# An encoder step on one core: w_out split by ACT and DVE, a shorter weight chain, w_down's maxima tied to their units, two token sums kept in SBUF

## The chip, the core and the metric

One core of a Trainium2 chip runs the whole program. Its engines are TensorE (PE, whose weight loads are shown apart as PEld), VectorE (DVE), ScalarE (ACT), GpSimd (POOL) and SyncE (SP, which here only issues DMA transfers). The metric is the device time of one execution in microseconds (us); lower is better. PE's clock is granted at one of two levels, 1.2 or 2.4 GHz; the profile gives the granted clock of a stretch as a share of the full one.

## The reference

One step of a one-layer streaming encoder on 2048 prompt tokens and 32 sample tokens, width 1024:

```python
h = h + rmsnorm(concat(y_conv, y_attn) @ W_out)
h = h + rmsnorm(relu(rmsnorm(h) @ W_up)**2 @ W_down)      # W_up 1024x4096, W_down 4096x1024
h = h + rmsnorm((p @ W_pe) * sigmoid(h @ W_g))

# differential attention, 4 heads, two softmax maps of each
a = softmax(where(visible, q k^T * scale - slope * |t - s|, -1e30))
attn = a[map 0] - lam * a[map 1]
o = rmsnorm(attn @ v, g_subln) * (1 - lam_init)
```

The attention is causal by chunks of 64 tokens; y_conv is a gated three-tap convolution.

## The kernel before, in words

Every large product is made in 16-bit floats with both operands as a high and a low half: the high half is the value rounded to 16 bits, the low half what is left, and three matmuls (high·high, low·high, high·low) go into one PSUM bank. So every weight and activation is split into halves on ACT (high, a copy with a scale, L170) and DVE (low, a scalar_tensor_tensor, L105). The weights are scaled by powers of two that come from their largest absolute value, so a reduction to the maximum stands before each split.

The program is written for a scheduler that sets the order of instructions on every engine from the dependences and from its own simulated timeline. What is written in another order, or depends on something else, can therefore move at many places.

The stages, with their time in the trace:
- 0 to 140 us: norm of the tokens and the first projections. 140 to about 975 us: attention, 4 heads of 16 units of 128 queries, woven with the other projections. A unit makes its scores (PE, L590, L591), adds the bias and takes the row maximum (DVE, L594), has the maximum negated on POOL (`nm`), exponentials with their row sums on ACT (L601), and then combines both maps. `weights_of` (L489) makes from the two row sums z1 and z2 a column of small [128,1] operations on POOL and DVE; ACT scales the second map with `sgc` (L625), DVE combines both (L105, `s<-s,sg,s`), PE transposes (`pta`), ACT and DVE split the transposed map (`at`), PE multiplies it by v (`smb`, L619, L621), and `subnorm` (L507) makes `rso` on POOL and `yg` on DVE.
- About 880 to 1135 us: 16 tiles of the product with w_out (`mix`, L897 to L901). Its eight blocks of rows are split by `split_in_place` (L175): POOL scales the block in place, ACT copies it to the high half (L176), POOL subtracts for the low half (L177). After the norm the tokens are transposed and combined to the seven sums of a Strassen-Winograd product, for two pairs of token groups. `place2` (L1206) puts the sums of the first pair (p = 0) into SBUF for good; those of the second pair go through a ring of 10 buffers (`ob`) to DRAM (`u2_d`).
- 1135 to 1777 us: w_up. 16 units, one for each block of 256 columns; a unit has two `up_pair` calls (one for each pair of tokens) of seven products, 12 matmuls each (L1301 to L1303), into a ring of three PSUM banks. `u2b` are the sums of the second pair, loaded back from DRAM (L1295). Beside unit k the `Piece` k+1 is made ready: load (`stg`), row maximum (`am`, L140), PE transpose of it (`pmx`), maximum (`p2mx`, L149), PE broadcast (`pmb`, L1154), scale (`um` to `i_u`), and the splits of the seven sums (`w7`, shown as `w`). `down_max` (L1370) loads a block of w_down (`stgd`) and reduces it to its largest absolute value (L1374); the table MAXIMA deals the 16 calls to units 2 to 13 in the order of the program text.
- 1777 to 2400 us: w_down. `raw` (L1450) loads a block, ACT and DVE split it to `v`; `fr` are the squared activations read back from DRAM, split to `hl`; L1533 to L1535 multiply. The buffers for `raw`, `fr` and `v` come from pools opened as those of the up stage close; `pva` lies in the place of the pool `pupa` (weights being prepared), the pools of `raw` and `fr` in that of `pupb`, whose `w7` the last matmuls of the up stage read.
- 2400 to 2627 us: the gate stage.

## Time and profile before

| | us |
|---|---|
| median of 3 runs | 2629.61 (2629.27 to 2631.32) |
| the profiled execution | 2628.69, of which the span of the records is 2626.9 |
| PE busy | 2532.1 (96% of the span) |
| DVE busy | 1692.2 (64%) |
| ACT busy | 1204.6 (46%) |
| POOL busy | 731.5 (28%) |

The span runs from the first to the last instruction; some 1.8 us lie outside it. PE is busy nearly all the time, so what can be found in such a profile are the stretches where PE stands (length less busy time) or runs with a granted clock below 1. Where PE stands, the list of waits says what it waited for last.

### The profile page before, as it was taken

The numbers are of one execution on the slowest core, as the hardware profiler recorded it, in microseconds if no ns is written. First come the engines' busy times: TensorE is split into PE (matmuls) and PEld (weight loads), VectorE is DVE, ScalarE is ACT, GpSimd is POOL, SyncE is SP. The second block draws the span as 40 slices with busy tenths as digits, with TensorE's granted clock in tenths as the row PEclk, the third lists the DMA queues.
The fourth block names the chain that finished last, engine by engine and source line by source line (L and its number), as shares of the span: only waits on it lengthen the run. The fifth ranks groups of instructions, "written<-read, shape, count | busy, mean of one in ns | idle before, by whom it ended". The sixth has DMA issues, their size and how long they took to land.

```text
span 2626.9 us, 42707 instructions
## 1 busy us (share of the span) xinstructions
PE 2532.1 (96%) x16495; PEld 1346.2 (51%) x16495; DVE 1692.2 (64%) x2933; ACT 1204.6 (46%) x2126; POOL 731.5 (28%) x1383
## 2 busy tenths in 40 slices
PE   8999999999999789989999999999999999999998
PEld 8755754755665444444444444443444444444454
DVE  6568858858887567886755555554563457555764
ACT  5446735744754545543343443444332223334553
POOL 2142233233222543432222222210220101233442
PEclk8999999999999899989999999999999999999999
DMA  5121111101111124577633333336753456541221
GB/s 174 50 66 38 38 33 45 52 28 57 46 62 33 61 73 153 173 279 267 205 129 124 117 125 129 117 142 243 253 194 107 145 206 225 197 139 57 93 75 60
DMA packets 215803, 315.76 MB, mean 120 GB/s; under 512 B 19184, under 2 KB 109712, under 8 KB 215600
## 3 DMA queue, kind: packets, MB, share of 16 engines
q1 hardware_dynamic: 215600, 313.04, 35.7%
q8 instruction: 129, 2.11, 0.3%
q14 instruction: 74, 0.61, 0.1%
HBM read 208.78 MB, written 100.02 MB: 118 GB/s over the span
## 4 chain that ended last, share of the span: by engine, by line
PE 61%; DVE 5%; DMA 5%; POOL 3%; ACT 2%; issue 1%; SPq 0%; DVEq 0%; POOLq 0%; ACTq 0%
PE mm L1533 6%; PE mm L1535 6%; PE mm L1534 6%; PE mm L1301 6%; PE mm L1303 6%; PE mm L1302 6%; PE mm L897 5%; PE mm L899 4%; PE mm L901 4%; DMA stgd<-in_w_down_dram 2%; PE lin L313 1%; PE lin L314 1%; PE lin L315 1%; DVE wdm L1374 1%; DMA wtmp<-in_w_pe_gate_dram 1%
## 5 line engine op out<-in xcount | busy, mean ns | idle before, releaser
L1533 PE MATMUL mm<-v,hl 128*128 128x512 f16 x896 | 340.1, 380 | 4.4 <-ACT v L170 4.4
L1535 PE MATMUL mm<-v,hl 128*128 128x512 f16 x896 | 339.9, 379 | 1.7 <-DVE hl L1495 1.5
L1534 PE MATMUL mm<-v,hl 128*128 128x512 f16 x896 | 340.0, 379 | 0.0
L313 PE MATMUL lin<-uh,whl 128*128 128x512 f16 (+1 forms) x832 | 265.6, 333 | 3.6 <-DVE ks L105 1.8
L314 PE MATMUL lin<-ul,whl 128*128 128x512 f16 (+1 forms) x832 | 265.4, 333 | 2.6 <-DVE ul L105 2.6
L315 PE MATMUL lin<-uh,whl 128*128 128x512 f16 (+1 forms) x832 | 265.2, 333 | 0.0
L1494 ACT ACTIVATE hl<-fr 128x1024 f16<-128x1024 f32 x112 | 117.5, 1051 | 319.9 <-PE mm L1535 302.5
L1495 DVE TENSOR_TENSOR hl<-fr,hl 128x1024 f16<-128x1024 f32 x112 | 144.7, 1299 | 178.1 <-ACT hl L1494 175.5
L601 ACT ACTIVATE s<-s,nm 128x128 f32<-128x128 f32 (+15 forms) x128 | 153.6, 1200 | 156.8 <-POOL nm L100 156.3
L1301 PE MATMUL mm<-u,w 128*128 128x512 f16 x448 | 171.0, 382 | 5.8 <-ACT w L170 3.8
L1301 PE MATMUL mm<-u2b,w 128*128 128x512 f16 x448 | 170.4, 382 | 2.4 <-DMA u2b<-u_d 1.3
L1302 PE MATMUL mm<-u2b,w 128*128 128x512 f16 x448 | 171.3, 382 | 0.0
L1302 PE MATMUL mm<-u,w 128*128 128x512 f16 x448 | 171.0, 382 | 0.0
L1303 PE MATMUL mm<-u,w 128*128 128x512 f16 x448 | 169.6, 381 | 1.2 <-DVE w L105 1.2
L1303 PE MATMUL mm<-u2b,w 128*128 128x512 f16 x448 | 169.9, 382 | 0.0
L1533 PEld LDWEIGHTS <-hl 128*128 128x128 f16 x896 | 87.7, 98 | 114.6 <-issue 11.0
L594 DVE CUSTOM_DVE_ANT_0 s<-sc,bias,mx 128x512 f32<-128x512 f32 (+3 forms) x192 | 135.4, 705 | 16.0 <-PE sc L591 10.8
L1535 PEld LDWEIGHTS <-hl 128*128 128x128 f16 x896 | 87.7, 98 | 109.2 <-DVE hl L1495 3.7
L1303 PEld LDWEIGHTS <-w 128*128 128x128 f16 x896 | 88.1, 98 | 108.1 <-issue 2.4
L1301 PEld LDWEIGHTS <-w 128*128 128x128 f16 x896 | 89.2, 100 | 105.0 <-ACT w L170 4.1
L1302 PEld LDWEIGHTS <-w 128*128 128x128 f16 x896 | 88.0, 98 | 104.5 <-issue 7.9
L1534 PEld LDWEIGHTS <-hl 128*128 128x128 f16 x896 | 87.7, 98 | 104.3 <-issue 0.9
(449 smaller groups left out, 6055.7 us busy)
## 6 DMA issues: line engine op xcount, KB each, us to landing
ff_d<-e SPq DMA_DIRECT2D x224, 256.0 KB, 2.0
fr<-ff_d SPq DMA_DIRECT2D x112, 512.0 KB, 4.3
raw<-in_w_down_dram SPq DMA_DIRECT2D x80, 512.0 KB, 4.5
xt<-in_x_prompt_dram SPq DMA_DIRECT2D x32, 512.0 KB, 4.1
stg<-in_w_up_dram SPq DMA_DIRECT2D x16, 1024.0 KB, 6.3
stgd<-in_w_down_dram SPq DMA_DIRECT2D x16, 1024.0 KB, 6.0
stg<-in_w_in_dram SPq DMA_DIRECT2D x24, 512.0 KB, 4.0
h_d<-ht SPq DMA_DIRECT2D x16, 512.0 KB, 2.9
```

The lines of the kernel that those rows point to most:

```text
L313: T.matmul(o, w[:, 0, ft], rh[:, ft, c], start=(ft == 0), stop=False)
L314: T.matmul(o, w[:, 0, ft], rl[:, ft, c], start=False, stop=False)
L315: T.matmul(o, w[:, 1, ft], rh[:, ft, c], start=False, stop=(ft == FT - 1))
L594: V.tensor_tensor_reduce(out=s_[:, c0:c0 + w_], in0=ps[:, :w_], in1=bias[:, b0:b0 + w_], scale=h["idd"], scalar=-BIG if prev is None else ...
L601: A.activation(out=s_[:, :nk], in_=s_[:, :nk], func=AF.Exp, bias=nm, accum_out=zz)
L1301: T.matmul(o, w[:, c, 0, kt], x[:, :, 0, kt], start=first and kt == 0, stop=False, skip_group_check=True)
L1302: T.matmul(o, w[:, c, 0, kt], x[:, :, 1, kt], start=False, stop=False, skip_group_check=True)
L1303: T.matmul(o, w[:, c, 1, kt], x[:, :, 0, kt], start=False, stop=kt == 3, skip_group_check=True)
L1495: V.tensor_tensor(out=hl[:, 1], in0=fr, in1=hl[:, 0], op=SUB)
L1533: T.matmul(ps, hl[:, 0, u % 2, c], v[:, 0], start=(u == 0), stop=False)
L1534: T.matmul(ps, hl[:, 0, u % 2, c], v[:, 1], start=False, stop=False)
L1535: T.matmul(ps, hl[:, 1, u % 2, c], v[:, 0], start=False, stop=(u == NU - 1))
```

## The change

- `weights_of`: before, 1/z2, then c = z1·nlam/z2 and 1 + alam·z1/z2, its reciprocal, and the product of both. After, d = z1·alam + z2, r = 1/d, sgc = z1·r·nlam, sg = z2·r. One DVE reciprocal and two POOL operations fewer in each of the calls.
- w_out's blocks go through `split` (L170 on ACT with the scale, L105 on DVE) in place of `split_in_place`.
- The second pair's sums for B11 and T3 have buffers of their own in SBUF (16 KB in each partition), and their stores to and loads from DRAM are gone (8 stores of 256 KB, 2 loads of 1 MB). The ring `ob` has 4 buffers in place of 10.
- The load of a `down_max` may be issued only after the store of A11 of the `up_pair` before it, its reduction only after that pair's S2 sum on DVE.
- `raw` has a ring of 3 and 1, and the first four blocks of w_down go into one buffer in `pva`; the ring of `v` changes accordingly.

```diff
     def weights_of(z1, z2, k0, rows=P):
-        rz, c, a_, sg = t1("rz"), t1("c"), t1("ca"), t1("sg")
-        V.reciprocal(out=rz[:rows], in_=z2[:rows])
-        ts(G, c[:rows], z1[:rows], rz[:rows], MUL, nlam[:rows], MUL)
-        ts(G, a_[:rows], rz[:rows], z1[:rows], MUL, alam[:rows], MUL)
-        ts(G, a_[:rows], a_[:rows], 1.0, ADD)
-        V.reciprocal(out=sg[:rows], in_=a_[:rows])
-        sgc = t1("sgc")
-        G.tensor_tensor(out=sgc[:rows], in0=sg[:rows], in1=c[:rows], op=MUL)
+        r, d, sg, sgc = t1("rz"), t1("ca"), t1("sg"), t1("sgc")
+        ts(G, d[:rows], z1[:rows], alam[:rows], MUL, z2[:rows], ADD)
+        V.reciprocal(out=r[:rows], in_=d[:rows])
+        ts(G, sgc[:rows], z1[:rows], r[:rows], MUL, nlam[:rows], MUL)
+        G.tensor_tensor(out=sg[:rows], in0=z2[:rows], in1=r[:rows], op=MUL)
         kk = t1("kk")
         if k0 is not None:
             ts(G, kk[:rows], sg[:rows], z1[:rows], MUL, k0[:rows], MUL)
...
         here["ppost"] = s_wo.enter_context(tc.tile_pool(name="ppost", bufs=1, reuse_waits="tile"))
         for r in ROWS:
             w = wo[r] = pwo.tile([P, 2, D], F16, tag="w", bufs=8, name="w")
-            split_in_place(w[:, 0], w[:, 1], out_scale["sgs"][r], out_scale["aswo" if r < 4 else "swo"])
+            split(w[:, 0], w[:, 1], out_scale["sgs"][r], out_scale["aswo" if r < 4 else "swo"])
             yield
...
     idn = cst.tile([P, 1], F32, name="idn")
     here["pupa"] = s_up.enter_context(tc.tile_pool(name="pupa", bufs=1, side="right", reuse_waits="tile"))
+    pu2r = s_up.enter_context(tc.tile_pool(name="pu2r", bufs=1, side="right", reuse_waits="tile"))
+    u2[1] = {c: pu2r.tile([P, 4, 2, 4, P], F16, name=f"u2b_{c}") for c in (B11, T3)}
+
     class Piece:
...
         def place2(p, c, i):
-            if p == 0:
-                o = u2[0][c][:, i]
-                return o, lambda: None
-            o = p3.tile([P, 2, 4, P], F16, tag="ob", bufs=10, name="ob")
+            if p == 0 or c in u2[1]:
+                return u2[p][c][:, i], lambda: None
+            o = p3.tile([P, 2, 4, P], F16, tag="ob", bufs=4, name="ob")
             return o, lambda: st(out=u2_d[c, i], in_=o.rearrange("p h t c -> p (h t c)"))
         def put2(p, c, i, src):
...
     pu2b = s_up.enter_context(tc.tile_pool(name="pu2b", bufs=1, side="right", reuse_waits="tile"))
     pev = s_up.enter_context(tc.tile_pool(name="pev", bufs=1, side="right", reuse_waits="tile"))
     e_ring = Ring((pmix, "q4", 3, 3), (pev, "e", 1, 1))
-    u2[1] = [None] * 7
-    for c in (B11, T3, T2, B21, T1, T4, B22):
+    for c in (T2, B21, T1, T4, B22):
         u2[1][c] = pu2b.tile([P, 4, 2, 4, P], F16, name=f"u2b_{c}")
         ld(out=u2[1][c].rearrange("p i h t c -> p i (h t c)"), in_=u2_d[c].rearrange("i p n -> p i n"))
     ys = psam.tile([P, NU, 2, DS], F32, name="ys")
...
         yield
         stt(e[A11], e[A11], 0.0, e[A11], MAX, MUL)
-        st(out=ff_d[A11, p, k], in_=e[A11])
+        here["sp"] = st(out=ff_d[A11, p, k], in_=e[A11]).ins
         A.activation(out=e[A22], in_=e[A22], func=AF.Relu)
         A.activation(out=e[A22], in_=e[A22], func=AF.Square)
         st(out=ff_d[A22, p, k], in_=e[A22])
...
         A.activation(out=e[S1], in_=e[S1], func=AF.Square)
         V.tensor_tensor(out=e[S3], in0=e[A11], in1=e[S1], op=SUB)
         V.tensor_tensor(out=e[S1], in0=e[S1], in1=e[A22], op=ADD)
-        V.tensor_tensor(out=e[S2], in0=e[S1], in1=e[A11], op=SUB)
+        here["dve"] = V.tensor_tensor(out=e[S2], in0=e[S1], in1=e[A11], op=SUB).ins
         G.tensor_tensor(out=e[S4], in0=e[A12], in1=e[S2], op=SUB)
         for c in (S3, S1, S2, S4):
             st(out=ff_d[c, p, k], in_=e[c])
...
     def down_max(k):
         sg = here["pupb"].tile([P, 2, D], F32, tag="stgd", bufs=1, name="stgd")
-        ld(out=sg, in_=w_down[0][k * 256:(k + 1) * 256].rearrange("(i p) c -> p i c", p=P))
-        yield
-        V.tensor_reduce(out=wdm[:, k:k + 1], in_=sg.rearrange("p i c -> p (i c)"), op=MAX, axis=AX.X, apply_absolute_value=True)
+        with tc.issue_after(here["sp"]):
+            ld(out=sg, in_=w_down[0][k * 256:(k + 1) * 256].rearrange("(i p) c -> p i c", p=P))
+        with tc.issue_after(here["dve"]):
+            V.tensor_reduce(out=wdm[:, k:k + 1], in_=sg.rearrange("p i c -> p (i c)"), op=MAX, axis=AX.X, apply_absolute_value=True)
     def w_down_scale():
...
         MAXIMA[2 + k * 11 // 15].append(k)
     for k in range(NU):
         make(k, 7)
-        dm = [down_max(i) for i in MAXIMA[k]]
-        for d in dm[:1]:
-            next(d)
         first = up_pair(k, 0)
...
         all_of(first)
         make(k + 1, 4)
-        for d in dm[:1]:
-            all_of(d)
+        for i in MAXIMA[k][:1]:
+            down_max(i)
         make(k + 1, 5)
-        for d in dm[1:]:
-            next(d)
         second = up_pair(k, 1)
...
         all_of(second)
         make(k + 1, 7)
-        for d in dm[1:]:
-            all_of(d)
+        for i in MAXIMA[k][1:]:
+            down_max(i)
         make(k + 2, 1)
         if k == NU - 2:
             w_down_scale()
...
     acc.update((t, pacc2.tile([P, D], F32, name=f"acc{t}")) for t in PTILES[14:])
     sres = pacc2.tile([DS, D], F32, name="sres")
     pt3 = s_t3.enter_context(tc.tile_pool(name="pt3", bufs=1, side="right", reuse_waits="tile"))
-    raw_ring = Ring((praw, "raw", 4, 4))
+    raw_ring = Ring((praw, "raw", 3, 3), (pva, "raw", 1, 1))
     fr_ring = Ring((pva, "fr", 2, 2), (pfr, "fr", 2, 2))
     hl_ring = Ring((pva, "hl", 2, 2), (pfr, "hl", 2, 2))
-    v_ring = Ring((pva, "v", 2, 1), (pmix, "q4", 3, 3), (pva, "v", 2, 1), (pv, "v", 6, 6))
+    v_ring = Ring((pva, "v", 1, 1), (pmix, "q4", 3, 3), (pv, "v", 7, 7))
     ORDER = [M1, M2, M6, M7, M5, M3, M4]
     vt = {}
     t3 = {}
...
     SAMPLE = {M1: 0, M2: 1, M7: 2, M3: 3}
-    def raw(i, j, k):
-        r = raw_ring.tile([P, 2, TG], F32, "raw")
+    def raw(i, j, k, first=False):
+        if first:
+            r = pva.tile([P, 2, TG], F32, tag="raw", bufs=1, name="raw")
+        else:
+            r = raw_ring.tile([P, 2, TG], F32, "raw")
         ld(out=r, in_=wdv[i, j][:, 2 * k:2 * k + 2])
         return r
...
         c = m[1]
         if c in (B11, B21, B22):
-            r = raw(*{B11: (0, 0), B21: (1, 0), B22: (1, 1)}[c], k)
+            r = raw(*{B11: (0, 0), B21: (1, 0), B22: (1, 1)}[c], k, c == B11 and k < 4)
         elif c == T2:
             b22, b12, r = raw(1, 1, k), raw(0, 1, k), raw(0, 0, k)
             t = t3[k] = pt3.tile([P, 2, TG], F32, tag="t3", bufs=8, name="t3")
```

What the edits move in the order of instructions stands in three places. First POOL, around the split of w_out before the change (`wst` are the blocks of w_out, `w` their halves, `nm` the negated row maxima of attention units, `rso` and `ca` small columns of such units):

```order
L102 TENSOR_SCALAR wst_12464<-wst_12464,aswo_12866 128x1024 x2
L177 TENSOR_TENSOR w_13273<-wst_12517,w_13273 128x1024
L177 TENSOR_TENSOR w_13304<-wst_12543,w_13304 128x1024
L100 TENSOR_SCALAR nm_13054<-mx_13052 128x1
L177 TENSOR_TENSOR w_13324<-wst_12580,w_13324 128x1024
L177 TENSOR_TENSOR w_13384<-wst_12597,w_13384 128x1024
L177 TENSOR_TENSOR w_13403<-wst_12416,w_13403 128x1024
L177 TENSOR_TENSOR w_13433<-wst_12447,w_13433 128x1024
L100 TENSOR_SCALAR nm_13148<-mx_13146 128x1
L177 TENSOR_TENSOR w_13444<-wst_12464,w_13444 128x1024
L177 TENSOR_TENSOR w_13497<-wst_12464,w_13497 128x1024
L102 TENSOR_SCALAR rso_13014<-sso_13012,kk_12946 128x1
```

After the change none of these large operations is left on POOL. The low halves stand on DVE instead, in a row with two scores of attention units between them (`s0` and `mx`, L591 in the changed file):

```order
L105 SCALAR_TENSOR_TENSOR w_13093<-wst_12349,i_wo_12693,w_13093 128x1024
L105 SCALAR_TENSOR_TENSOR w_13120<-wst_12375,i_wo_12693,w_13120 128x1024
L591 ISA s0_12960,mx_12964<-sc_12961,bias_1537,idd1_9584 128x512
L591 ISA mx_12964 128x1
L105 SCALAR_TENSOR_TENSOR w_13139<-wst_12412,i_wo_12693,w_13139 128x1024
L105 SCALAR_TENSOR_TENSOR w_13198<-wst_12429,i_wo_12693,w_13198 128x1024
L591 ISA s0_12960,mx_12969<-sc_12966,bias_1537,mx_12964,idd1_9584 128x512
L591 ISA mx_12969 128x1
L105 SCALAR_TENSOR_TENSOR w_13216<-wst_12251,aswo_12695,w_13216 128x1024
L105 SCALAR_TENSOR_TENSOR w_13242<-wst_12279,aswo_12695,w_13242 128x1024
L105 SCALAR_TENSOR_TENSOR w_13252<-wst_12296,aswo_12695,w_13252 128x1024
L105 SCALAR_TENSOR_TENSOR w_13304<-wst_12296,aswo_12695,w_13304 128x1024
```

So the eight low halves move from POOL to DVE, and the small operations that stood between and behind them on POOL no longer have them ahead; a unit's scores on DVE now do.

Second DVE at the start of the up stage, before (`wdm` is a maximum of w_down, `ob` sums of the second token pair, `pt1` to `pt3` parts of such sums, `e0` to `e5` evacuated products of unit 0, `p2mx`, `um`, `e_u`, `ux` the scale of piece 1):

```order
L1374 TENSOR_REDUCE wdm_14075<-stgd_16770 128x1
L1255 TENSOR_TENSOR pt2_15698<-ptr_15707,pt1_15697 128x512
L149 TENSOR_REDUCE p2mx_15932<-pmx_15930 1x1
L1341 TENSOR_TENSOR e5_15765<-e0_15762,e1_15763 128x512
L100 TENSOR_SCALAR um_15936<-pmb_15934 128x1
L105 SCALAR_TENSOR_TENSOR ob_15714<-ptr_15707,i_g2_13550,ob_15714 128x512
L1342 TENSOR_TENSOR e1_15763<-e1_15763 128x512
L100 TENSOR_SCALAR e_u_15937<-um_15936 128x1
L102 TENSOR_SCALAR ux_15942<-um_15936,g2_m_13544 128x1
L105 SCALAR_TENSOR_TENSOR ob_15719<-pt3_15699,i_g2_13550,ob_15719 128x512
L105 SCALAR_TENSOR_TENSOR ob_15723<-pt2_15698,i_g2_13550,ob_15723 128x512
L1343 TENSOR_TENSOR e4_15764<-e1_15763,e0_15762 128x512
```

One reduction stands here two rows ahead of `p2mx`, and sums `ob` of the second pair stand in between. After the change, at the same place:

```order
L105 SCALAR_TENSOR_TENSOR u2b_5_13873<-pt3_15478,i_g2_13353,u2b_5_13873 128x512
L105 SCALAR_TENSOR_TENSOR ob_15493<-ptr_15486,i_g2_13353,ob_15493 128x512
L105 SCALAR_TENSOR_TENSOR ob_15500<-pt2_15477,i_g2_13353,ob_15500 128x512
L105 SCALAR_TENSOR_TENSOR ob_15504<-pt1_15476,i_g2_13353,ob_15504 128x512
L149 TENSOR_REDUCE p2mx_15705<-pmx_15703 1x1
L105 SCALAR_TENSOR_TENSOR ob_15508<-kept_15456,i_g2_13353,ob_15508 128x512
L1339 TENSOR_TENSOR e5_15538<-e0_15535,e1_15536 128x512
L1340 TENSOR_TENSOR e1_15536<-e1_15536 128x512
L1341 TENSOR_TENSOR e4_15537<-e1_15536,e0_15535 128x512
L100 TENSOR_SCALAR um_15709<-pmb_15707 128x1
L100 TENSOR_SCALAR e_u_15710<-um_15709 128x1
L102 TENSOR_SCALAR ux_15715<-um_15709,g2_m_13347 128x1
```

The reduction is gone from the place (four more lay close by, before and behind the piece shown, and are gone too); `u2b_5` stands where an `ob` stood, and most of the sums stand ahead of `p2mx`.

Third DVE in a unit in the middle of the up stage, before, from the sums of a pair (`e5`, `e1`, `e4`) through the scale of the next piece (`um` to `i_u`, `ut`):

```order
L1341 TENSOR_TENSOR e5_17452<-e0_17449,e1_17450 128x512
L1342 TENSOR_TENSOR e1_17450<-e1_17450 128x512
L100 TENSOR_SCALAR um_17623<-pmb_17621 128x1
L1343 TENSOR_TENSOR e4_17451<-e1_17450,e0_17449 128x512
L100 TENSOR_SCALAR e_u_17624<-um_17623 128x1
L102 TENSOR_SCALAR ux_17629<-um_17623,g2_m_13544 128x1
L102 TENSOR_SCALAR i_u_17627<-e_u_17624 128x1
L1161 RECIPROCAL ut_17630<-ux_17629 128x1
```

Nothing of w_down stands here. After the change, in such a unit with a reduction (`stgd` is the loaded block of w_down):

```order
L1339 TENSOR_TENSOR e5_17223<-e0_17220,e1_17221 128x512
L1340 TENSOR_TENSOR e1_17221<-e1_17221 128x512
L100 TENSOR_SCALAR um_17394<-pmb_17392 128x1
L1341 TENSOR_TENSOR e4_17222<-e1_17221,e0_17220 128x512
L100 TENSOR_SCALAR e_u_17395<-um_17394 128x1
L102 TENSOR_SCALAR ux_17400<-um_17394,g2_m_13347 128x1
L1373 TENSOR_REDUCE wdm_13863<-stgd_17412 128x1
L102 TENSOR_SCALAR i_u_17398<-e_u_17395 128x1
L1161 RECIPROCAL ut_17401<-ux_17400 128x1
L100 TENSOR_SCALAR ut_17401<-ut_17401 128x1
```

The reduction now stands between the scale's first steps and `i_u`, ahead of the splits of the next piece; the 16 of them are spread from unit 2 on, one or two in a unit.

On SP, the loads of `stgd` move from among the stores and loads of the second pair's sums to the units, each behind a store of A11; five loads of `u2b` stand where seven did; and four loads of `raw` for the first product of the down stage stand among the stores of the last two units of the up stage, where before the first of them stood behind the last unit's stores of A11, A12 and A22.

## Rows read from the trace of the kernel before

**Rows 1.** windows: length, busy PE, PEld, DVE, ACT, POOL, PEclk, DMA share, GB/s

```profile
140.00:860.00 720.00, 699.38 (x5834) 436.38 (x5833) 554.55 (x1354) 404.17 (x782) 213.23 (x651) 1.00 0.15 44
860.00:950.00 90.00, 67.64 (x458) 41.16 (x457) 58.06 (x152) 52.13 (x99) 50.58 (x96) 0.89 0.23 71
...
1100.00:1200.00 100.00, 89.69 (x502) 42.16 (x500) 73.05 (x92) 46.73 (x87) 34.05 (x44) 0.93 0.75 265
1200.00:1300.00 100.00, 95.65 (x520) 43.12 (x519) 76.54 (x92) 36.45 (x60) 23.01 (x20) 0.97 0.67 225
...
1400.00:1600.00 200.00, 200.00 (x1200) 92.67 (x1199) 114.91 (x168) 78.25 (x128) 53.59 (x46) 1.00 0.37 127
...
1760.00:1800.00 40.00, 34.81 (x160) 14.76 (x159) 24.28 (x33) 23.30 (x35) 3.81 (x3) 0.96 0.71 263
```

**Rows 2.** what PE waited for in the attention stage: us in total, times, longest

```profile
PE smb L619 <- ACT at L170: 3.9, 5, 1.8
```

**Rows 3.** groups of POOL, 140:860 us: count, busy, mean ns, idle before

```profile
L102 POOL TENSOR_SCALAR c<-z,rz,nlam 128x1 f32<-128x1 f32 x53 | 19.7, 371 | 75.5 <-DVE rz L492 75.0
```

**Rows 4.** timeline of POOL, 885 to 920 us: start, length, line, operation, [idle before]

```profile
886.81 4.83 POOL L102 TENSOR_SCALAR wst<-wst,i_wo 128x1024 f32<-128x1024 f32 x4
...
913.09 0.28 POOL L102 TENSOR_SCALAR rso<-sso,kk 128x1 f32<-128x1 f32 x1
```

**Rows 5.** timeline of DVE, 885 to 935 us

```profile
891.94 0.75 DVE L594 CUSTOM_DVE_ANT_0 s<-sc,bias,idd 128x512 f32<-128x512 f32 x1 [0.43 <-PE pta L632]
...
914.75 0.35 DVE L100 TENSOR_SCALAR yg<-smb,rso 128x128 f32<-128x128 f32 x1 [12.76 <-POOL rso L513]
```

**Rows 6.** the tile whl (first projections): ns min/median/max, first and last start

```profile
L170 ACT ACTIVATE whl<-stg,i_w x24: 1132/1147/1167, 13.3 to 833.5; 128x1024 f16<-128x1024 f32 x24
L105 DVE SCALAR_TENSOR_TENSOR whl<-stg,i_w,whl x24: 1264/1284/2149, 14.4 to 834.8; 128x1024 f16<-128x1024 f32 x24
```

**Rows 7.** timeline of PE, first units of the up stage

```profile
1156.21 0.38 PE L1302 MATMUL mm<-u,w 128*128 128x512 f16 x1
1156.42 0.38 PE L1303 MATMUL mm<-u,w 128*128 128x512 f16 x1
...
1157.06 0.27 PE L147 MATMUL pmx<-ident,am 128*1 128x128 f32 x1
...
1166.17 0.61 PE L1301 MATMUL mm<-u,w 128*128 128x512 f16 x1 [3.25 <-ACT w L170]
```

**Rows 8.** what PE waited for, 1000 to 1320 us

```profile
PE pmb L1154 <- DVE p2mx L149: 7.6, 3, 3.6
```

**Rows 9.** line 1374, reductions over w_down: ns min/median/max, first and last start

```profile
L1374 DVE TENSOR_REDUCE wdm<-stgd x16: 2266/2286/2289, 1139.2 to 1289.6; 128x1 f32<-128x2048 f32 x16
```

**Rows 10.** DMA issues, 1100:1300 us: count, KB each, median us to landing

```profile
stgd<-in_w_down_dram SPq DMA_DIRECT2D x16, 1024.0 KB, 6.0
...
u2b<-u_d SPq DMA_DIRECT2D x7, 1024.0 KB, 14.6
```

**Rows 11.** timeline of DVE in a unit in the middle of the up stage

```profile
1482.32 0.69 DVE L105 SCALAR_TENSOR_TENSOR e<-e 128x512 f32<-128x512 f32 x1
...
1490.85 0.69 DVE L1343 TENSOR_TENSOR e<-e,e 128x512 f32<-128x512 f32 x1
...
1506.15 2.29 DVE L140 TENSOR_REDUCE am<-stg 128x1 f32<-128x2048 f32 x1 [4.97 <-DMA stg<-in_w_up_dram]
```

**Rows 12.** timeline of DVE, 1685 to 1690 us

```profile
1686.13 0.75 DVE L105 SCALAR_TENSOR_TENSOR w<-s3t,i_u,w 128x512 f16<-128x512 f32 x1
1686.80 1.75 DVE L105 SCALAR_TENSOR_TENSOR w<-stg,i_u,w 128x512 f16<-128x512 f32 x1
```

**Rows 13.** timeline of POOL, 1685 to 1690 us

```profile
1686.30 1.70 POOL L1190 TENSOR_TENSOR stg<-stg 128x512 f32<-128x512 f32 x1
```

**Rows 14.** timeline of PE at the end of the up stage

```profile
1781.87 1.63 PE L1533 MATMUL mm<-v,hl 128*128 128x512 f16 x4 [4.41 <-ACT v L170]
```

**Rows 15.** timeline of ACT at the end of the up stage

```profile
1781.09 2.65 ACT L170 ACTIVATE v<-raw,swd 128x512 f16<-128x512 f32 x4 [2.25 <-DMA raw<-in_w_down_dram]
```

## The prediction

> **What bounds the kernel now.** I read the windows by stage first, and in each row two numbers: the length less PE's busy time, and the granted clock. Their sum is what the stretch loses against a PE that never stands and always has its full clock: idle time, plus length times (1 − clock). The reader is to see that the kernel is bound by PE and that the losses sit in four places [rows 1]. In the middle of the up stage nothing is lost (200.00 us busy of 200.00, clock 1.00). The attention stage (140 to 860) loses 720.00 − 699.38 = 20.6 us, at full clock. 860 to 950, where w_out is split beside the last attention units, loses 90.00 − 67.64 = 22.4 us idle and 90 × 0.11 = 9.9 of clock, 32.3 together. The start of the up stage loses 10.3 + 7.0 in 1100 to 1200 and 4.4 + 3.0 in 1200 to 1300, 24.7 together. The passage to the down stage (1760 to 1800) loses 5.2 + 1.6 = 6.8. The five edits lie in these four places and add work only to stretches where PE loses nothing. Second I read, place by place, the timelines of the engines PE waits for.
>
> **A, the weight chain in attention.** Each call loses one DVE reciprocal and two POOL operations of a [128,1] column, of which the nearest row says 0.37 us for one [rows 3]; the same row shows POOL standing 75.0 us over 53 calls for DVE's reciprocal, so a hop between these engines is on each call's chain. Off PE's path that is worth nothing. What PE is seen to wait for behind this chain is the transposed map, 3.9 us in 5 waits [rows 2]. The bounds: a gain of up to those 3.9 us, or, because every unit's small operations move, a loss of as much again. I take a gain of 2, nearer to the gain, since the chain only gets shorter.
>
> **B, the split of w_out.** POOL scales and subtracts the eight blocks from 886.81 until the first small operation behind them, `rso`, starts at 913.09 [rows 4]. `rso` is what DVE waits for: it stands idle for 12.76 us, 902.0 to 914.75 [rows 5], and the unit's chain and PE stand with it. After the change, ACT makes the high halves and DVE the low ones, in a form and shape that the first projections already use: 1.147 and 1.284 us each [rows 6]. ACT's eight take 8 × 1.147 = 9.2 us and begin as early as POOL's did. DVE is free of its earlier work at 891.94 − 0.43 = 891.5 [rows 5]; its eight take 8 × 1.284 = 10.3, and the two scores that stand between them 2 × 0.8 = 1.6, so the last low half ends at about 891.5 + 11.9 = 903.4, and `rso` no longer has any of it ahead on POOL. The restart that `yg` marks moves from 914.75 to 903.4 at best: 11.3 us. What DVE did between 891.9 and 902.0 now comes behind the splits; without the two scores already counted that is at most 10.1 − 1.6 = 8.5 us, which leaves a gain of 2.8 if all of it is on the path. Most of it belongs to units whose `nm` then waited on POOL until 913, so I take 10, nearer to 11.3. Upwards, about half of the stretch's clock loss could come back: 11.3 + 5 = 16. Ends: 3 and 16.
>
> A rule that speaks against this edit can be weighed in the trace. A split on DVE of 128x512 takes 0.75 us, and the next one of the same form 1.75 us while POOL runs a 1.70 us operation over the same stretch [rows 12, 13]. The Trainium skill, in "SBUF — State Buffer", section "SBUF: two separate sides", says that a DVE operation with two SBUF inputs and a GpSimd operation share a port pair as an exclusive lock, the loser blocked for the other's whole instruction. By that rule, with which these rows agree, each small POOL operation on a unit's chain could wait out a 1.28 us split; four of them would take 5 us off B's 10.
>
> **C, the start of the up stage.** Sixteen reductions of 2.29 us stand on DVE between 1139.2 and 1289.6 [rows 9], 36.6 us, and DVE also waits for their loads. They stand ahead of the `p2mx` of the next piece's scale, for which PE waits 7.6 us in 3 waits [rows 8], and of its splits: from `pmx` at 1157.06 to the next matmul of the next unit at 1166.17 it is 9.1 us, nearly all idle [rows 7]. The clock of the two windows is 0.93 and 0.97 [rows 1]. After the change no reduction stands there, and PE has the products of the two sums kept in SBUF to do while the piece's scale is made: in the order, 23 matmuls between `pmx` and `pmb`, at 0.21 us each [rows 7] 4.9 us. The chain of 9.1 loses at least the one reduction in it, 6.8 left, of which 4.9 is covered: about 2 us of waiting stay. I allow 1 us for the first of the five sums that still come by DRAM, where a load took 14.6 us in the median [rows 10], and 2 for the clock behind such a gap. Of 24.7 lost, 5 remain: a gain of 20. Ends: everything comes back, 24.7; or the first window keeps its whole 17.3 because the chain and the loads stay as late as they are, and the gain is 7.4.
>
> **The reductions in their new place.** They cost DVE 16 × 2.29 = 36.6 us in units 2 to 13, plus a wait if a load is late. What hides it: in the middle stretch DVE is busy 114.91 of 200 us [rows 1], and its standing 4.97 us for a load ahead of `am` [rows 11] left PE without any idle time in that window. The loads are tied to the A11 store, which follows DVE's 1482.32 + 0.69 = 1483.0, and the reduction to the S2 sum, done at 1490.85 + 0.69 = 1491.5: 8.5 us apart, against 6.0 from issue to landing [rows 10, 11]. So I cost them at 0; with no cover it would be the 36.6.
>
> **D, the first blocks of w_down.** PE waits 4.41 us for the first `v` [rows 14], and the window loses 6.8 with its clock. With the block loaded and split before the last matmul of the up stage that wait goes. Late next is ACT, which now makes `v` in the last units ahead of an evacuation; one `v` half is 2.65 / 4 = 0.66 us [rows 15], and two of them ahead of an evacuation cost 1.3 us. The clock comes back in part. I take 4. Ends: 0, if `hl` is as late as `v` was, and 6.8.
>
> **The sum.** 2 + 10 + 20 + 4 = 36 us less, against the profiled execution's 2628.69: 2592.7. The median of the runs shown, 2629.61, is 0.9 above that execution, so the forecast is 2593.6, or 2594 rounded.
>
> **Rivals.**
> 1. Slower: the reductions in the units. If `stgd` lands as `u2b` did, 14.6 us after its issue, it is 6.1 us later than the 8.5 at which DVE reaches it; with the reduction DVE then stands 8.4 us, where a stand of 4.97 is known to be covered. The other 3.4 us reach PE through late evacuations, 16 times: 55 us more, 2594 + 55 = 2649. It decides from a landing later than 8.5 + 4.97 − 2.29 = 11.2 us after the issue. For it: loads did take that long at the start of the up stage, with DMA 0.75 busy. Against it: in the middle stretch DMA is 0.37 busy [rows 1], and the reductions are where it is quiet.
> 2. DVE becomes the bound at w_out: its pushed-back work lands on the units' path, and small POOL operations wait beside the splits. B gives 3 in place of 10: 2601. For it: DVE has no idle time from 891.9 on, by that order; against it: it had 12.76 us idle right behind.
> 3. The start of the up stage stays bound by the piece's own chain and the DRAM sums: C gives 7.4 in place of 20, 2594 + 12.6 = 2606. For it: only one of the reductions lies between `pmx` and the first matmul; against it: the rest had pushed the work before them back as well.
> 4. The ties do nothing and the reductions crowd elsewhere: that is rival 3 without C's gain, 2614; against it is the order, in which the first one stands in unit 2.
>
> **How the numbers follow.** The forecast as it stands, each term within its ends, has 0.72; rival 2 has 0.10, rival 3 0.10, rival 4 0.02, rival 1 0.04, and 0.02 is left for a stage I expect nothing of, attention above all, in which a new order costs as much as the rest gains. All terms at their good ends give 3.9 + 16 + 24.7 + 6.8 = 51.4 and 2578; rivals 2 and 3 together give 2614. I take 2577 to 2614. A measurement of this kernel can tell about 0.2% (5 us) from no change. Faster by more than that: forecast, rivals 2, 3 and 4 and a little less, 0.93; within it 0.03; slower 0.04.
>
> **What would show it.** In the profile after: no idle time near 13 us of DVE behind w_out, and POOL's row without 128x1024 operations (B); PE idle in 1100 to 1300 near 3 us rather than 14.7, clock above 0.98, the reductions spread over some 450 us without stands of DVE beyond 2 us ahead of them (C); the first L1533 with a wait under 1 us (D); PE idle in attention within 4 us of 20.6 (A). The forecast is wrong if windows in units 2 to 13 show PE idle time, if the stretch 860 to 950 still loses over 28 us, or if `pmb` still waits as long in the first unit.

## The result and the profile after

The changed kernel takes 2602.2 us in the median of 4 runs (2600.3 to 2605.3), the kernel before beside it 2630.5 (2629.3 to 2633.4): a ratio of 0.9892, 95% interval 0.9875 to 0.9909, or 28.3 us less. The forecast was 2594 with a range of 2577 to 2614.

The same windows as [rows 1], of the profile after (columns as there), and one more near the end of the down stage:

```profile
140.00:860.00 720.00, 692.89 (x5794) 435.64 (x5791) 540.24 (x1279) 405.17 (x777) 204.85 (x589) 0.99 0.16 44
860.00:950.00 90.00, 75.68 (x541) 44.59 (x542) 75.72 (x182) 58.01 (x115) 34.37 (x92) 0.96 0.24 74
1100.00:1200.00 100.00, 98.85 (x557) 46.89 (x556) 70.02 (x101) 49.57 (x92) 32.44 (x45) 0.98 0.54 194
1200.00:1300.00 100.00, 100.00 (x559) 46.56 (x558) 63.63 (x85) 40.65 (x66) 27.98 (x23) 1.00 0.46 152
1400.00:1600.00 200.00, 200.00 (x1156) 92.80 (x1155) 121.87 (x171) 78.91 (x128) 51.51 (x47) 1.00 0.49 163
1760.00:1800.00 40.00, 40.00 (x206) 17.06 (x205) 21.93 (x26) 21.03 (x29) 0.00 (x0) 1.00 0.81 290
2200.00:2360.00 160.00, 153.62 (x719) 68.10 (x717) 84.03 (x86) 51.08 (x63) 42.22 (x30) 0.98 0.42 146
```

and that last window in the kernel before:

```profile
2200.00:2360.00 160.00, 158.26 (x762) 69.74 (x761) 99.82 (x104) 54.20 (x64) 54.30 (x30) 1.00 0.57 194
```

Read as losses (idle, and length times one less the clock), the stretch 860 to 950 fell from 32.3 us to 14.3 + 3.6 = 17.9, the start of the up stage from 24.7 to 1.2 + 2.0 = 3.2, and the passage to the down stage from 6.8 to nothing. Two stretches lost more than before: attention, where PE's idle time rose from 20.6 to 27.1 us and the clock in its row fell from 1.00 to 0.99 (7.2 us, by the rounded figures), and 2200 to 2360, from 1.7 to 6.4 with a clock of 0.98, where nothing had been expected.

Windows cut at fixed times mix what was shifted, so the rest goes by marks: the start of the first score, of the transpose of w_out's maxima (`pmx` from `wc`, the last step ahead of w_out's scale), of the first w_up matmul, of the last w_down matmul, and the end. Lengths between them in each profiled execution, in us, beside the median time:

```text
kernel                               attention  mix   up+down  gate | median  ratio to before [95% interval]
before                                 734.7   252.4  1249.6  242.1 | 2630.5
changed                                743.4   238.9  1226.7  242.3 | 2602.2  0.9892 [0.9875, 0.9909]
e1  changed, old weights_of            733.5   242.8  1232.5  242.2 | 2598.6  0.9875 [0.9861, 0.9889]
e2  before, new weights_of             743.2   250.8  1249.0  242.1 | 2636.2  1.0029 [1.0017, 1.0041]
e3  before, w_out on ACT and DVE       736.0   243.5  1253.3  242.1 | 2623.4  0.9971 [0.9960, 0.9983]
e4  before, first blocks early         735.5   254.0  1253.2  242.1 | 2631.3  1.0002 [0.9994, 1.0011]
e5  before, maxima tied                735.6   254.1  1227.4  242.1 | 2608.2  0.9906 [0.9886, 0.9925]
e6  before, two sums in SBUF           735.5   254.0  1244.9  242.2 | 2624.5  0.9976 [0.9966, 0.9987]
e7  changed, d on DVE                  755.1   242.1  1226.2  242.3 | 2615.2  0.9933 [0.9916, 0.9950]
e8  changed, hl first                  742.5   239.5  1223.1  242.5 | 2594.9  0.9856 [0.9839, 0.9873]
e9  changed, reductions twice          745.3   239.1  1229.9  242.7 | 2603.3  0.9890 [0.9875, 0.9905]
e10 before, c written later            731.8   253.2  1252.3  242.3 | 2633.8  1.0004 [0.9996, 1.0013]
e11 changed, sg written first          747.6   240.7  1226.0  242.3 | 2606.0  0.9906 [0.9893, 0.9920]
e12 changed, old weights_of, hl first  734.6   243.4  1226.1  242.2 | 2590.6  0.9849 [0.9836, 0.9863]
```

The experiments ran in three groups (e1 to e4, e5 to e8, e9 to e12), each beside runs of the kernel before (medians 2630.8, 2631.6 and 2632.4). A ratio goes by its own group; a difference in us from the changed kernel crosses groups and is uncertain by one or two us.

By these marks the change is +8.7 in attention, -13.5 in the mix stage and -22.9 from the first w_up to the last w_down matmul. Up to the second mark PE, DVE, ACT and POOL each run the same operations in the same order in the seven kernels with the old weights_of as it was, and so they do in the four with the new one as it is. Where that order is the same, the length repeats within 3 us: 733.5 to 736.0 in the seven, 742.5 to 745.3 in the four. So the 8.7 us are a difference between two orders and not the spread of runs. e7, e10 and e11 each have an order of their own.

In the mix stage, DVE's timeline of the changed kernel (start, length, operation, [idle before]) shows the low halves in their new place:

```profile
897.81 2.48 DVE L105 SCALAR_TENSOR_TENSOR w<-wst,i_wo,w 128x1024 f16<-128x1024 f32 x2
...
904.00 4.87 DVE L105 SCALAR_TENSOR_TENSOR w<-wst,aswo,w 128x1024 f16<-128x1024 f32 x4
908.96 0.16 DVE L493 RECIPROCAL rz<-ca 128x1 f32<-128x1 f32 x1
```

and POOL's, in the same stretch, what the small operations beside them took:

```profile
897.98 1.18 POOL L100 TENSOR_SCALAR nm<-mx 128x1 f32<-128x1 f32 x1 [1.25 <-DVE mx L591]
904.17 1.18 POOL L100 TENSOR_SCALAR nm<-mx 128x1 f32<-128x1 f32 x1 [5.01 <-DVE mx L591]
906.19 2.74 POOL L102 TENSOR_SCALAR ca<-z,alam,z 128x1 f32<-128x1 f32 x1 [0.83 <-ACT s L598]
909.23 0.34 POOL L102 TENSOR_SCALAR sgc<-z,rz,nlam 128x1 f32<-128x1 f32 x1 [0.31 <-DVE rz L493]
```

The idle 12.76 us of [rows 5] are gone. `ca` takes 2.74 us beside the low halves and `sgc`, an operation of the same form, 0.34 behind them; `nm` takes 1.18 beside one, 0.22 alone. The excess is 2.4 + 2 × 0.96 = 4.3 us. What it cost is another matter: `rz`, which needs `ca`, stands behind the last low half on DVE in any case and starts 0.09 us after it, so the wait of `ca` cost next to nothing.

The Trainium skill, "SBUF — State Buffer", section "SBUF: two separate sides", has the loser of the shared port pair blocked for the other's whole instruction. The two `nm` agree with that: each ends with the low half beside which it began. `ca` does not: it began during the second of the four low halves of its row and ended only with the fourth (908.87), so it waited through more than one instruction.

What PE waited for longest between 1000 and 1320 (us in total, times, longest), against [rows 8]:

```profile
PE mm L1299 <- ACT w L170: 1.1, 1, 1.1
```

PE no longer waits for `p2mx`. The reductions (duration in ns, first and last start), against [rows 9], have no idle time of DVE ahead of them; their blocks landed 5.6 us after the issue in the median:

```profile
L1373 DVE TENSOR_REDUCE wdm<-stgd x16: 2275/2277/2280, 1236.0 to 1656.1; 128x1 f32<-128x2048 f32 x16
```

In the kernel before, DVE stood for these loads too, between 1130 and 1300 (all of them use one buffer, so a load waits for the reduction before it):

```profile
DVE wdm L1374 <- DMA stgd<-in_w_down_dram: 17.0, 9, 4.2
```

Near the end of the down stage PE waits for a split `hl`. Its timeline, then those of ACT, DVE and POOL:

```profile
2289.87 0.61 PE L1530 MATMUL mm<-v,hl 128*128 128x512 f16 x1 [3.43 <-ACT hl L1491]
```

```profile
2287.32 1.06 ACT L1604 ACTIVATE q<-acc 128x1024 f32<-128x1024 f32 x1 [5.17 <-DVE acc L1630]
...
2288.78 3.88 ACT L1491 ACTIVATE hl<-fr 128x1024 f16<-128x1024 f32 x4
```

```profile
2281.02 3.15 DVE L105 SCALAR_TENSOR_TENSOR wg<-wtmp,i_wg,wg 128x1024 f16<-128x1024 f32 x1
2284.09 3.14 DVE L1630 TENSOR_TENSOR acc<-acc,q 128x1024 f32<-128x1024 f32 x1
```

```profile
2279.99 6.16 POOL L177 TENSOR_TENSOR wg<-wtmp,wg 128x1024 f16<-128x1024 f32 x2
```

Four `hl` stand on ACT behind the square of the first gate tile (`q`), which waits 5.17 us for `acc` on DVE. There a split of a gate weight takes 3.15 us and `acc` 3.14, beside 6.16 us of POOL; the split's form took 1.28 in [rows 6]. In the kernel before, four `hl` stand behind the same `q`, but `q` waits only 1.21 us and `acc` takes 1.21:

```profile
2317.94 1.06 ACT L1607 ACTIVATE q<-acc 128x1024 f32<-128x1024 f32 x1 [1.21 <-DVE acc L1633]
```

```profile
2316.63 1.21 DVE L1633 TENSOR_TENSOR acc<-acc,q 128x1024 f32<-128x1024 f32 x1
```

So the queue on ACT is not new; new is that `acc` comes late. This goes with the edit of the first blocks of w_down: `q` waits 1.21 us in each of the six traces without that edit (before, e2, e3, e5, e6, e10) and 5.17 in each of the six that have it without a further tie (changed, e1, e4, e7, e9, e11), where PE then stands 3.3 to 3.4 us.

### The profile page after: what moved, and what is told of

It reads as the page before. It is cut to its first block, busy times and chain, and to the rows that moved or that the text cites. A ratio compares the mean times of both kernels' runs of the same rounds, so it can differ in the third digit from the quotient of the medians.

```text
span 2598.6 us, 42548 instructions
## 1 busy us (share of the span) xinstructions
PE 2520.6 (97%) x16495; PEld 1343.5 (52%) x16495; DVE 1677.6 (65%) x2873; ACT 1208.8 (47%) x2126; POOL 689.7 (27%) x1299
## 4 chain that ended last, share of the span: by engine, by line
PE 66%; DVE 4%; ACT 2%; DMA 2%; issue 2%; POOL 1%; DVEq 0%; POOLq 0%; SPq 0%; ACTq 0%
PE mm L1299 8%; PE mm L1301 7%; PE mm L1300 7%; PE mm L1530 6%; PE mm L1532 6%; PE mm L1531 6%; PE mm L894 4%; PE mm L896 4%; PE mm L898 4%; PE lin L315 1%; PE lin L314 1%; PE lin L313 1%; DMA wtmp<-in_w_pe_gate_dram 1%; DVE s L591 1%; PE ptr L185 1%
## 5 line engine op out<-in xcount | busy, mean ns | idle before, releaser
L591 DVE CUSTOM_DVE_ANT_0 s<-sc,bias,mx 128x512 f32<-128x512 f32 (+3 forms) x192 | 134.9, 703 | 19.9 <-PE sc L588 15.5
```

The source lines that it names most:

```text
L591: V.tensor_tensor_reduce(out=s_[:, c0:c0 + w_], in0=ps[:, :w_], in1=bias[:, b0:b0 + w_], scale=h["idd"], scalar=-BIG if prev is None else ...
```

## The experiments

**e1 and e2: the weight chain undone, and alone.**

```diff
-        ts(G, d[:rows], z1[:rows], alam[:rows], MUL, z2[:rows], ADD)
-        V.reciprocal(out=r[:rows], in_=d[:rows])
...
+        V.reciprocal(out=rz[:rows], in_=z2[:rows])
+        ts(G, c[:rows], z1[:rows], rz[:rows], MUL, nlam[:rows], MUL)
```

(e1; e2 is the kernel before with the opposite edit.) Expected of e1 and of e2:

> The changed kernel with the old weights_of (edit A undone, the other four edits kept). Theory 1, the shorter chain's version of the attention stage costs 8 us: the scale of w_out's maxima (pmx of wc), at 890.7 us in the changed kernel, is back near 883, waits of PE for the row maxima fall from 12.3 to about 6.5 us, and the time is 2602 - 8 = 2594 (2591 to 2597). Theory 2, the 8 us come from something else or from the spread of runs: 2600 to 2604.

> The kernel before with the new weights_of alone. Theory 1: slower by about 8 us in attention, some of it perhaps taken up around 900 us where work waits for POOL anyway: 2634 to 2639. Theory of the prediction (a gain of 2, ends -4 and +4): 2626 to 2634, nearest 2628.

Measured: 2598.6 and 2636.2. The attention window of e1, then of e2:

```profile
140.00:860.00 720.00, 698.08 (x5843) 435.97 (x5841) 554.56 (x1356) 406.05 (x784) 211.99 (x653) 1.00 0.15 44
2200.00:2360.00 160.00, 150.93 (x691) 66.47 (x690) 80.63 (x82) 49.14 (x60) 42.12 (x30) 0.96 0.41 137
```

```profile
140.00:860.00 720.00, 692.09 (x5794) 435.19 (x5793) 540.92 (x1280) 404.88 (x777) 204.40 (x589) 0.99 0.15 44
```

The attention stage follows the chain: 733.5 with the old one, 743.2 with the new one, PE's idle time there 21.9 and 27.9. PE's waits for the row maxima (`mx`, 140 to 880 us) go the same way, 8.1 us before, 12.3 in the changed kernel and 8.8 in e1, where about 6.5 was expected. Alone the new chain costs 5.4 us. e1's 2598.6 lies between the bands of its two theories: it gains only 3.6 in the median (the intervals of e1 and of the changed kernel overlap), not 8. The marks show why: its mix stage is 3.9 longer than in the changed kernel, and PE stands longer at the end of the down stage (150.93 busy of 160.00, clock 0.96). Attention and mix together, the new chain costs 6.0 (changed against e1) and 6.9 (e2 against before).

**e3: w_out alone.**

```diff
-            split_in_place(w[:, 0], w[:, 1], out_scale["sgs"][r], out_scale["aswo" if r < 4 else "swo"])
+            split(w[:, 0], w[:, 1], out_scale["sgs"][r], out_scale["aswo" if r < 4 else "swo"])
```

> The kernel before with w_out split by ACT and DVE alone. From the traces of before and after (13.5 us less between pmx of wc and the first matmul of the up stage): 2617. The prediction's term: 10 less, 2620. The rival in which DVE becomes the bound there: 3 less, 2627.

Measured: 2623.4, 7.4 less; 8.9 less in the mix stage. DVE's last four low halves, and `yg`:

```profile
897.69 4.87 DVE L105 SCALAR_TENSOR_TENSOR w<-wst,aswo,w 128x1024 f16<-128x1024 f32 x4
...
911.23 0.34 DVE L100 TENSOR_SCALAR yg<-smb,rso 128x128 f32<-128x128 f32 x1
```

The low halves end at 902.6, where the prediction had 903.4. `yg`, whose start the prediction took for the restart, comes at 911.23, 3.5 us earlier than before and not 11.3: pushed-back work stands ahead of it, as the sum had allowed. The gain lies between the prediction's term and the rival; its interval (4.5 to 10.5 us) holds the 10 and not the 3. The 13.5 taken from the marks did not come: see the account of B below.

**e4: the first blocks of w_down alone.**

```diff
-            r = raw(*{B11: (0, 0), B21: (1, 0), B22: (1, 1)}[c], k)
+            r = raw(*{B11: (0, 0), B21: (1, 0), B22: (1, 1)}[c], k, c == B11 and k < 4)
```

(and the rings that go with it.)

> The kernel before with the first blocks of w_down early alone. The prediction's term: 4 less, 2626. Theory that the edit brings its 6.8 us at the passage but moves the preparation of the gate weights so that hl stands behind it near the end of the down stage (some 8 us, as in the profile after): 2630 to 2632, with PE waits for hl of over 5 us. If that stall is not this edit's: 2623 to 2625.

Measured: 2631.3, ratio 1.0002. Windows, then what PE waits for from 1740 to 2400:

```profile
1740.00:1800.00 60.00, 59.88 (x334) 26.93 (x334) 30.89 (x44) 28.94 (x43) 6.39 (x4) 1.00 0.67 230
2200.00:2360.00 160.00, 152.10 (x716) 66.23 (x715) 101.58 (x103) 52.23 (x61) 48.87 (x30) 0.97 0.55 188
```

```profile
PE mm L1538 <- DVE hl L1498: 4.6, 2, 3.8
PE mm L1536 <- ACT hl L1497: 3.3, 1, 3.3
```

The passage loses nothing any more, and 7.9 us of idle time with a clock of 0.97 stand near the end of the stage, with the same wait of `q` for `acc` (5.17 us) as in the changed kernel: the second theory.

**e5 and e6: the maxima alone, the sums alone.**

```diff
+        with tc.issue_after(here["sp"]):
+            ld(out=sg, in_=w_down[0][k * 256:(k + 1) * 256].rearrange("(i p) c -> p i c", p=P))
+        with tc.issue_after(here["dve"]):
```

```diff
-            if p == 0:
+            if p == 0 or c in u2[1]:
```

> The kernel before with the maxima of w_down tied to their units, alone. Theory 1, the reductions are what holds DVE at the start of the up stage: some 15 of the 24.7 us lost in 1100 to 1300 come back, 2630.8 - 15 = 2616 (2613 to 2619), the waits for p2mx (7.6 us) fall below 4, and PE waits about 1 to 2 us for u2b. Theory 2, it is mostly the second pair's sums on their way through DRAM: 2625 to 2629. If the reductions cost anything in their new place, the windows 1300 to 1740 show PE idle time beyond 2 us.

> The kernel before with the sums for B11 and T3 of the second pair kept in SBUF, alone. Theory 1 (the reductions hold DVE): only the wait for u2b (1.3 us) and what 23 matmuls (5 us) can cover of the 9.1 us behind pmx: 2624 to 2628. Theory 2 (the way through DRAM holds PE): 2612 to 2619.

Measured: 2608.2 (23.4 less) and 2624.5 (7.1 less). Windows of e5, then of e6, and e6's longest waits of PE in 1000 to 1320:

```profile
1100.00:1200.00 100.00, 97.37 (x554) 46.21 (x555) 71.86 (x103) 51.08 (x95) 32.35 (x46) 1.00 0.63 226
1200.00:1300.00 100.00, 100.00 (x559) 46.44 (x557) 64.52 (x90) 39.93 (x65) 26.90 (x26) 1.00 0.46 155
```

```profile
1100.00:1200.00 100.00, 92.51 (x520) 43.36 (x521) 76.73 (x101) 50.29 (x92) 31.98 (x43) 0.97 0.68 238
1200.00:1300.00 100.00, 94.65 (x524) 43.54 (x522) 74.79 (x98) 37.94 (x62) 28.11 (x27) 0.98 0.67 228
```

```profile
PE pmb L1157 <- DVE p2mx L149: 4.7, 1, 4.7
PE mm L1302 <- ACT w L170: 4.6, 1, 4.6
```

With the reductions moved away, 2.6 us of loss are left, with the sums still on their way through DRAM. With the sums in SBUF and the reductions where they were, PE still waits 4.7 for `p2mx` and 4.6 for the split. The first theory holds, with more gain than it gave: 2608.2 lies below its band of 2613 to 2619. The edit moves the loads of the blocks as well, for which DVE had stood 17.0 us; how much of the gain is the reductions and how much their loads is not separated by any run.

**e7: d on DVE.**

```diff
-        ts(G, d[:rows], z1[:rows], alam[:rows], MUL, z2[:rows], ADD)
+        ts(V, d[:rows], z1[:rows], alam[:rows], MUL, z2[:rows], ADD)
```

> The changed kernel with d = z1*alam + z2 of weights_of made on DVE in place of POOL, so that the reciprocal behind it no longer waits for POOL. Theory 1, the new chain loses because DVE, which works in order, stands 30.5 us for POOL's d ahead of other units' scores: the attention stage (first score to pmx of wc, 743.4 us in the changed kernel, 734.7 before) falls to 735 to 739 and the time to 2594 to 2598. Theory 2, the loss is the scheduler's other order of everything, with no one wait behind it: the attention stage comes out anywhere between 733 and 748, with no relation to this wait.

Measured: 2615.2, 13 us more than the changed kernel; attention 755.1. DVE's waits in the chain (140 to 880 us), in the kernel before, the changed kernel and e7:

```profile
DVE rz L492 <- ACT s L601: 19.9, 21, 2.1
DVE sg L496 <- POOL ca L100: 17.5, 22, 1.5
```

```profile
DVE rz L493 <- POOL ca L102: 30.5, 29, 2.4
```

```profile
DVE ca L102 <- ACT s L598: 25.0, 18, 2.3
```

DVE stands less in the chain from kernel to kernel (37.4, 30.5, 25.0 us), while the stage grows (734.7, 743.4, 755.1). So neither the hop to POOL nor DVE's standing in the chain as a whole explains the loss. The first theory falls, and 755.1 lies even outside the band given with the second. Part of e7's own loss has a cause that can be named: DVE stands 7.37 us for a late load of a w_out block ahead of its maximum, and PE then 4.56 us.

**e8: hl first.**

```diff
+        late = here["hl", len(BLOCKS) - 5] if t == TILES[0] else None
+        with (tc.issue_after(late) if late is not None else ExitStack()):
+            V.tensor_tensor(out=ff, in0=ff, in1=ht[:rows], op=ADD)
+        s_, inv = tokscale(ff, rows, D, xt[:rows], late)
```

> The changed kernel with the square of the first gate tile (q of acc, L1604 on ACT) and the sum before it on DVE tied behind the fourth block's hl of the last product, so that they no longer stand ahead of four hl. Theory 1, the early start of the down stage is given back near its end because these four hl queue on ACT behind an operation that waits 5.2 us for DVE: the idle time in 2200 to 2360 falls from 6.4 to about 2 us, its clock from 0.98 to 1.00, and the time is 2595 (2593 to 2598). Theory 2, hl is late for another reason (its loads, or DVE): 2600 to 2604.

Measured: 2594.9, 7.3 us less than the changed kernel. The window, and ACT's timeline:

```profile
2200.00:2360.00 160.00, 154.64 (x735) 69.41 (x734) 86.80 (x89) 53.82 (x69) 39.39 (x34) 1.00 0.44 147
```

```profile
2282.59 1.99 ACT L1491 ACTIVATE hl<-fr 128x1024 f16<-128x1024 f32 x2
...
2293.48 1.06 ACT L1605 ACTIVATE q<-acc 128x1024 f32<-128x1024 f32 x1 [5.41 <-DVE acc L1633]
```

```profile
PE mm L1532 <- DVE hl L1492: 5.4, 3, 2.7
```

The `hl` begin 5 us earlier (counted from the first w_up matmul), ahead of `q`, and the clock stays at 1.00. PE's idle time falls only from 6.4 to 5.4, not to 2 (DVE's halves of `hl` are the wait now, the last lines), so most of the gain of the stage (3.6 us by the marks) is clock, and the rest of the 7.3 lies outside the stage or in the spread of runs. The first theory holds for the time, not for the idle time.

**e9: the reductions twice.**

```diff
             V.tensor_reduce(out=wdm[:, k:k + 1], in_=sg.rearrange("p i c -> p (i c)"), op=MAX, axis=AX.X, apply_absolute_value=True)
+            V.tensor_reduce(out=wdm[:, k:k + 1], in_=sg.rearrange("p i c -> p (i c)"), op=MAX, axis=AX.X, apply_absolute_value=True)
```

> The changed kernel with each of the 16 reductions over w_down done twice in its place, 36.6 us more on DVE in units 2 to 13. Theory 1, the new place is covered with room to spare: the windows 1200 to 1740 stay without idle time of PE and the time at 2600 to 2605. Theory 2, the cover is thin (DVE is in order, and evacuations and the next piece's splits stand behind the reductions): each unit loses 1 to 2.3 us, 2618 to 2639.

Measured: 2603.3. The window over the units, and the added reductions:

```profile
1200.00:1740.00 540.00, 540.00 (x3144) 251.03 (x3143) 368.36 (x486) 223.11 (x362) 143.34 (x124) 1.00 0.47 158
```

```profile
L1374 DVE TENSOR_REDUCE wdm<-stgd x16: 2270/2274/2286, 1244.7 to 1659.6; 128x1 f32<-128x2048 f32 x16
```

DVE has 16 × 2.274 = 36.4 us more to do there and PE is busy 540.00 of 540.00: the first theory. (The loads are not doubled.)

**e10 and e11: one line of the chain moved.**

```diff
-        ts(G, c[:rows], z1[:rows], rz[:rows], MUL, nlam[:rows], MUL)
         ts(G, a_[:rows], rz[:rows], z1[:rows], MUL, alam[:rows], MUL)
         ts(G, a_[:rows], a_[:rows], 1.0, ADD)
+        ts(G, c[:rows], z1[:rows], rz[:rows], MUL, nlam[:rows], MUL)
```

(e10, on the kernel before; e11 swaps `sgc` and `sg` in the changed one.)

> The kernel before with one line of the old weights_of moved: c is written behind 1 + alam*z1/z2 in place of ahead of it; the same operations, and nothing waits longer for anything. The scheduler orders attention anew. Theory 1, the attention stage's length is set by the scheduler's order as a whole, which any edit there redraws: it differs from the 733.5 to 736.0 us of the old chain by more than 3 us, one way or the other. Theory 2, it is set by the chain's own operations: 733 to 737, and the time is 2628 to 2633.

> The changed kernel with one line of the new weights_of moved: sg = z2*r is written ahead of sgc in place of behind it, so that ACT's scaling waits one POOL operation of 0.2 us longer in each call. Theory 1 (the order as a whole): an attention stage that differs from the 743 us of the new chain by more than 3 us, either way. Theory 2 (the chain's own operations): 743 to 748 and 2602 to 2607.

Measured: attention 731.8 and 747.6, times 2633.8 and 2606.0. e11's is 4.2 from the changed kernel's, as the first theory has it, and just inside the second's band; e10's is 1.7 to 4.2 below the old chain's others. e11's shift has one cause that its trace names, a wait of DVE for a load of w_out that the changed kernel does not have, and PE's stand right behind it:

```profile
852.61 1.22 DVE L841 TENSOR_REDUCE wmax<-wst 128x1 f32<-128x1024 f32 x1 [7.87 <-DMA wst<-in_w_out_dram]
```

```profile
854.73 0.29 PE L618 MATMUL smb<-vhl,at 128*128 128x128 f16 x1 [4.55 <-DVE at L105]
```

The changed kernel has no such stand: its longest wait of PE in that stage is 2.3 us, so what it loses against the kernel before is spread over many short waits and the clock. Inconclusive: moving one line shifts the stage by a few us, but in none of the runs is a new chain shorter than 742 or an old one longer than 736.

**e12: both together.** The edits of e1 and e8.

> The changed kernel with the old weights_of and with the first gate tile's square tied behind four hl (the two edits that gained, together). If the gains add: 2602.2 - 8.5 (attention back at 735) - 7.3 = 2586. If the down stage's end gives part of it back, as with the old chain alone: 2590 to 2593.

Measured: 2590.6, the lowest median of all (its interval overlaps that of e8), 11.6 us below the changed kernel; the gains do not quite add, as the second expectation had it.

```profile
140.00:860.00 720.00, 699.18 (x5838) 437.24 (x5836) 554.31 (x1355) 405.81 (x784) 212.19 (x653) 1.00 0.16 44
2200.00:2360.00 160.00, 153.95 (x720) 68.77 (x718) 84.53 (x88) 53.41 (x69) 41.37 (x37) 0.98 0.41 141
```

Attention is back at 20.8 us of idle time, and the end of the down stage still loses 6.1. Against e1 the tie of `q` shortens the stretch from w_up to w_down by 6.4 us, where e8 had 3.6 against the changed kernel: it gains in both.

## Why the prediction was right, and where it was not

The time lies in the range, 8 us above the forecast, but not as the forecast had it: A lies outside its ends, and some of what A and D miss is made up by B and C, which brought more than their terms. That the errors partly cancel is luck. Of the signs that the prediction named, those of B, C and D came (17.9 us lost in 860 to 950, 1.2 idle in 1100 to 1300, no wait at the passage); that of A did not (27.1 us idle in attention, 6.5 from the 20.6). The terms, by the single edits and by the marks:

- **C**, forecast 20: right in mechanism and near in size. 22.9 us by the marks with D in it, which alone brings nothing. e5 shows that the reductions with their loads carry it (23.4 us alone); the sum priced one reduction in the chain and named the loads, but gave DVE's 17.0 us of standing for them no price. The part of the step that gave the two sums in SBUF a share (PE covered by 23 matmuls, a wait left for the DRAM sums) was not needed: e5 without them leaves 2.6 us of loss, less than the 5 forecast. The sums alone gain 7.1; beside the tied maxima little seems left for them (1227.4 by the marks in e5, 1226.7 in the changed kernel), but no run has the two without D.
- **The reductions in their new place**, forecast 0: right, shown by e9 with twice as many. Rival 1 did not happen: no reduction waits for its load, which lands after 5.6 us where the rival needed more than 11.2.
- **B**, forecast 10: right within its ends. 7.4 alone; 13.5 by the marks in the changed kernel, of which 3.9 is what the new chain's attention gives back there (with the old chain on both sides it is 9.6 in e1 and 8.9 in e3). The last low half came within a microsecond of where the sum put it (e3); the restart of `yg` did not, since pushed-back work stood ahead of it. Small POOL operations did wait beside the splits, 4.3 us in sum against the 5 that had been feared; the longest of these waits was hidden, and what the others cost is not shown.
- **D**, forecast 4: wrong, 0 (e4, at the lower of its ends). The step said that the wait at the passage goes and named ACT's evacuations as what is late next. The wait went and the evacuations cost nothing; what was late next lay 500 us further on. In every trace with the edit `q` waits 4 us longer for `acc` than in every trace without it, and PE stands for the `hl` behind it unless `q` is tied (e8, e12). Those two show that this queue costs time: with `q` behind four `hl` that stand of PE is gone and the stretch is 3.6 and 6.4 us shorter, though PE still waits for DVE's halves of `hl`. Why `acc` is late is only argued: it and the split ahead of it run beside 6.16 us of POOL and take 2.95 us longer than before (6.29 in place of 3.34), and no run takes POOL's work away. The prediction had no term for this place, where PE stood for 1.7 us in 160; idle time did not say how much slack there was.
- **A**, forecast a gain of 2 with ends of -4 and +4: wrong, and outside its ends. The step said "nearer to the gain, since the chain only gets shorter". e1 and e2 show attention 8 to 10 us longer with the new chain, 6 to 7 with the mix stage behind it, 5.4 in the time when alone. The step that failed is the bound: the loss was priced by the one wait that the chain was seen to cause (3.9 us), where the edit redraws the order of the whole 740 us stage. Why the redrawn order is worse stays open: DVE's standing in the chain falls while the stage grows (e7), and e10 and e11 show shifts of 2 to 4 us by a moved line. Two orders with the old chain and three with the new one are too few to say whether 8 is chance of that kind or the new chain's own.

By the marks, A misses by 10.7 and D by 4; B and C brought some 6 more than their terms; that makes the 8 us. The single edits add up to +5.4 - 7.4 - 23.4 - 7.1 + 0.5 = -32.0, against -28.3 measured together.

## What to carry to other kernels

Where a scheduler sets the order, price an edit in a long stage that is almost without idle time as a redraw of that stage, whatever the edit itself saves, and try it alone. The five orders of this 740 us stage spread over 23 us (731.8 to 755.1), and the shorter chain came with the longer ones. Where a stall is removed, look for the next place at which the engine meets work that it does not set the pace of, however far on, and ask for the slack there, not for the idle time. Here 36 us of added work cost nothing on an engine that had a third of its time free in a steady stage (e9), and the same work, with loads to wait for, cost 23 us in a stretch where that engine was the one waited for (e5).

## What the runs showed of the hardware

A POOL operation on a [128,1] column, 0.34 us by itself, took 2.74 us beside a row of DVE operations of 1.28 us with two inputs in SBUF, until the last of them ended (908.87), and a DVE operation of 128x1024 3.15 us instead of 1.28 beside POOL's. Near the end of the down stage PE stood for 3.43 us until 2289.87; its granted clock was 1.00 from 2280 to 2288.9, 0.50 (the lower level) from 2289.1 to 2295.7 and 1.00 again behind. Over the 160 us that makes 0.98, 3.2 us of loss. In e8, with 5.4 us of idle time in pieces of at most 2.7, the clock was 1.00.
